# Ordering edges in a hybrid encoder layer: bias tiles behind a row's scaling, and the second half of a mix behind the first half's low parts

## The chip, the cores and the metric

The kernel runs on one core of one Trainium2 chip. A core has five engines that run their own instruction lists side by side: PE (TensorE, matrix products; PEld is its weight load), DVE (VectorE), ACT (ScalarE), POOL (GpSimd) and SP (SyncE, which here only issues transfers, as ACT does for some). Matrix products write to PSUM, a small memory of eight banks; everything else lies in SBUF, and transfers between SBUF and the main memory go through 16 DMA engines. The metric is the time of one execution on the device in microseconds (us); smaller is better.

## The reference, cut to what matters

One encoder layer on 1024 tokens of 1024 channels, in float32: a normalised input goes through one projection whose columns feed two attention groups side by side; their outputs are normalised apart, joined, projected back and added to the input; a gated MLP with a small convolution follows.

```python
hn = rmsnorm(h, norm_mix[l])
proj = jnp.einsum('bsd,de->bse', hn, w_in[l])
qa, ka, va, qb, kb, vb = jnp.split(proj, splits, axis=-1)
...
o_a = window_gqa_sink(qa, ka, va, sink[l])            # 8 heads, window of 128 tokens
o_b = neighbourhood_attention(qb, kb, vb, rpb[l])     # 8 heads, 8 x 16 window on the 16 x 64 grid
mix = jnp.concatenate([rmsnorm(o_a, norm_a[l]), rmsnorm(o_b, norm_b[l])], axis=-1)
h = h + jnp.einsum('bse,ed->bsd', mix, w_out[l])
hn = rmsnorm(h, norm_ffn[l])
h = h + conv_gated_mlp(hn, w_gate[l], w_up[l], conv_w[l], conv_b[l], w_down[l])
return rmsnorm(h, norm_final)
```

In the neighbourhood attention each head adds a learned bias to its scores, taken from a small table by the row and column offset of query and key:

```python
bias = rpb32[:, row_off][:, :, col_off]
s = jnp.einsum('bchd,bicjhd->bhcij', q_r, k_win).astype(jnp.float32) * scale + bias[None]
p = jax.nn.softmax(s.reshape(B, B_HEADS, GRID_W, kh * NA_KW), axis=-1)
```

## The kernel before, in words

**Precision.** Each float32 operand of a product is split into a high part (a rounded copy, made by ACT) and a low part (what is left, made by DVE or POOL); a product is three matmuls, high by high, high by low and low by high. So a matmul of a new operand waits for an ACT instruction and then for a DVE or POOL one.

**Order of the work.** A planner at compile time orders each engine's list; at run time an engine works its list strictly from the front, and a wait at the front holds all behind it. The planner goes by priorities: earlier in the program is more urgent, `tc.high_priority(offset=n)` lifts instructions by n places, and `behind(name)` adds an edge for the order alone: what is traced in its block on the marked instruction's engine comes behind that instruction. PE is different: its order is the order of the program, written by hand (`manual_schedule`). A generator (`filler`) deals out the steps of the projections between those of the attention, so that PE always has a product to work on while softmax goes on elsewhere.

**Attention of group B** (heads 0 to 7, the grid). A head has eight blocks of 128 queries, called rows here, b = 0 to 7. The function `units_grid` gives for each a step `q_step(b)`: the scores (PE, L434), then `softmax`: DVE adds the bias and takes the minimum (L464), ACT takes the exponential with its sum (L468), DVE the reciprocal `sm` (L469). From there a row goes one of two ways by its letter in PATH_B, "QQTQQQTQ". On path T (rows 2 and 6) POOL scales the row (L472), PE transposes it (L496), and ACT and DVE write its high and low parts (L499, L500). On path Q ACT writes the high part (L483), POOL scales a copy (L488) and writes the low part (L489), and a transposing transfer on SP's queue turns both (L490). Then PE multiplies by the values (L598). Up to three units of two rows run ahead of the products that use them.

**Bias tiles.** `bias_tiles(h)` loads head h's part of the table (`rr`, one buffer, L546, on SP's queue) and POOL subtracts it from two masks (L556, 128 x 384, and L557, 128 x 256) into `xb` (two buffers). It is called for head h+1 in `q_step(4)` of head h, and for head 0 early, at unit 8 of group A. Nothing but data and buffers sets when the planner places these two.

**Hand-over.** After the last head: `scale_gains`, the squared sums of group B's four mix tiles and their inverse roots (`vb2`, per token half). Three rows of the output projection's first half (`OutA`, d = 5 to 7, L685 adds the residual) still run as filler. The second heads' mix is then normalised in place (L1129, DVE), copied to a high part (L1130, ACT) and reduced to a low part (L1131, DVE), for token half h = 0 and then h = 1, four tiles each. ACT also squares the eight first raw tiles of the MLP's weights to find their scale (`head_scan`, L1068), and `settle_scales` sums the results (L1035). Then come sixteen products, `product16(ps, wo[d], mg[4:8], h)`, all d with half 0 first, then all d with half 1; `settle_out` adds their results to the residual (L1207). `load_wo` prepares their weights; the low parts (L1104) of d >= 2 stand behind "rows", the last low part of half 0.

The core of the hand-over before the change:

```python
for h in range(2):
    wide = widen(vb2[h], "pt")
    for i in range(4):
        ...
        nc.vector.scalar_tensor_tensor(x, x, gains[:, 4 + i:5 + i], wide, op0=ALU.mult, op1=ALU.mult)
        nc.scalar.activation(hi, x, AF.Copy)
        copied = nc.vector.tensor_tensor(lo, x, hi, op=ALU.subtract)
```

Of the kernel before, what the change touches and what calls it, by code (L numbers as in the profile page):

```python
# [18 lines left out]
ALU = mybir.AluOpType  # L19
# [44 lines left out]
def hybrid_layer(tc, xT, w_in, w_out, w_gate, w_up, w_down, small, sink, rpb, consts, rope, out):  # L64
    nc = tc.nc
    with ExitStack() as ctx:
# [192 lines left out]
        def widen(v, tag, n=4):  # L259

            wide = bank("sw", tag)
            for c in range(n):
                nc.tensor.transpose(wide[:, c * 128:(c + 1) * 128], v[:, c:c + 1].to_broadcast([128, 128]), ident)
            return wide
# [185 lines left out]
        class Rows:  # L450
# [5 lines left out]
            def softmax(self, path, j, ps, n, bias, nsink=None, skip=0):  # L456

                c = n // 128
                with tc.high_priority(offset=50):
                    p = apool.tile([128, 386], F32, name="p", tag="p", bufs=PS)  # L460
                    nm, sm = (spool.tile([128, 1], F32, name=x) for x in ("nm", "sm"))
                    if nsink is not None:
                        nc.gpsimd.tensor_copy(p[:, n:n + 1], nsink)
                    nc.vector.tensor_tensor_reduce(  # L464
                        out=apart(p[:, 0:n]), in0=apart(ps[:, 0:n]), in1=bias, scale=1.0, scalar=3e38 if nsink is None else nsink,
                        op0=ALU.add, op1=ALU.min, accum_out=nm)
                    e = n if nsink is None else n + 1
                    nc.scalar.activation(p[:, 0:e], p[:, 0:e], AF.Exp, bias=nm, scale=-1.0, accum_out=sm)  # L468
                    nc.vector.reciprocal(sm, sm)  # L469
                    x = apart(p[:, 0:n])  # L470
                    if path in "PT":
                        nc.gpsimd.tensor_scalar(x, x, sm, P_TOP, op0=ALU.mult, op1=ALU.mult)  # L472
                    if path == "T":
                        return lambda: self.turn(j, p, c, skip)
                    hl = staged()
                    hi, lo = (hl[:, 0:c, s] for s in range(2))
                    if path == "P":
                        nc.scalar.activation(hi, x, AF.Copy)
                        nc.gpsimd.tensor_tensor(lo, x, hi, op=ALU.subtract)
                    else:  # L480
                        by = spool.tile([128, 1], F32, name="by")
                        nc.vector.tensor_scalar(by, sm, P_TOP, None, op0=ALU.mult)
                        nc.scalar.activation(hi, x, AF.Copy, scale=by)  # L483
                        if path == "D":
                            nc.vector.scalar_tensor_tensor(lo, x, by, hi, op0=ALU.mult, op1=ALU.subtract)
                        else:
                            y = apart(apool.tile([128, 384], F32, name="y", tag="y", bufs=YS)[:, 0:n])
                            nc.gpsimd.tensor_scalar(y, x, sm, P_TOP, op0=ALU.mult, op1=ALU.mult)  # L488
                            nc.gpsimd.tensor_tensor(lo, y, hi, op=ALU.subtract)  # L489
                    mark["flip"] = nc.sync.dma_start(self.tile[:, j, skip:skip + c].rearrange("p i s q -> p (i s) q"), hl[:, 0:c], transpose=True)  # L490
# [51 lines left out]
        def bias_tiles(h):  # L542

            raw = apool.tile([128, RAW_LEN], F32, name="rr", tag="rr", bufs=1)
            src = bass.AP(tensor=rpb.tensor, offset=rpb.offset + h * RPB_LEN, ap=[[RPB_W, ROWS], [1, 8], [1, RAW_LEN]])
            nc.sync.dma_start(raw, src)  # L546
            x = apool.tile([128, 5, 128], F32, name="xb", tag="xb")
            a = raw[:, 0:1]
            view = lambda d0, step, n: bass.AP(
                tensor=a.tensor, offset=a.offset + RAW_LEN - 1 - 8 * (d0 + 1),  # L550
                ap=[list(a.ap[0]), [-8 * step, n], [-RPB_W, ROWS], [-1, 8]])
            mk = cst[:, K_MB:K_MB + 384].rearrange("p (v r c) -> p v r c", r=ROWS, c=8)
            far = mk[:, 1:2]
            far = bass.AP(tensor=far.tensor, offset=far.offset, ap=[list(far.ap[0]), [0, 2], [8, ROWS], [1, 8]])
            xv = x[:, :, :].rearrange("p v (r c) -> p v r c", c=8)
            nc.gpsimd.tensor_tensor(xv[:, 1:4], mk, view(-1, 1, 3), op=ALU.subtract)  # L556
            nc.gpsimd.tensor_tensor(xv[:, 0::4], far, view(-1, 2, 2), op=ALU.subtract)  # L557
            return x

        bias_of = {}  # L560
# [98 lines left out]
        class OutA:  # L659
# [9 lines left out]
            def run(self):  # L669
                d = self.d  # L670
                if d < 6:
                    h1[d] = big("h1", "mix" if d < 4 else "op")
                    xt = tmp("xr")
                    nc.sync.dma_start(xt, xT[d])
                else:
                    for e in range(d, KT):
                        if h1[e] is None:
                            h1[e] = big("h1", "op")
                            mark["xr"] = nc.sync.dma_start(h1[e], xT[e])
                    xt = h1[d]  # L680
                for h in range(2):
                    ps = bank("pj", "pj")
                    yield from product16(ps, self.w, mg[0:4], h)
                    with tc.high_priority(offset=500):
                        nc.vector.scalar_tensor_tensor(h1[d][:, tsl(h)], ps, wo_back, xt[:, tsl(h)], op0=ALU.mult, op1=ALU.add)  # L685

            def post(self):
# [216 lines left out]
        def fill(n):  # L904
            while n > 0 and next(filler, False):
                n -= 1
# [122 lines left out]
        def settle_scales(i, n, tag):  # L1029

            fs = FO[i:i + n]
            n = len(fs)
            rows = (w_rows if i >= HEAD else head_rows)[:, 2 * i:2 * i + 2 * n].rearrange("p (n s) -> p n s", s=2)
            v = small("wv", 4)[:, 0:n]
            nc.vector.tensor_tensor(v, rows[:, :, 0], rows[:, :, 1], op=ALU.add)  # L1035
            s = measure(v, tag)
            back = little(4, "back", "backs", 4)[:, 0:n]
            nc.vector.reciprocal(back, s)  # L1038
            nc.gpsimd.tensor_tensor(back, back, unit_back.to_broadcast([128, n]), op=ALU.mult)  # L1039
            for j, f in enumerate(fs):  # L1040
                taps = little(3, "taps", "taps", 12)
                nc.gpsimd.tensor_scalar(taps, par[:, C_CW + 3 * f:C_CW + 3 * f + 3], back[:, j:j + 1], 1.0, op0=ALU.mult, op1=ALU.mult)
                scale_of[f], back_of[f], taps_of[f] = s[:, j:j + 1], back[:, j:j + 1], taps
# [21 lines left out]

        def head_scan(i, j):
            junk = big("junk", "op")
            nc.scalar.activation(junk[:, :].rearrange("p (k c) -> p k c", c=128), head_raw[FO[i]][j], AF.Square, accum_out=head_rows[:, 2 * i + j:2 * i + j + 1])  # L1068

        W = {}  # L1070

# [24 lines left out]
        def load_wo(d, pools):  # L1096
            raw = wo_raw.pop(d)
            if d % 2 == 0:
                wo_raw["t"] = big("wo", "op").bitcast(F16)[:, :].rearrange("p (d s j c) -> p d s j c", d=2, s=2, c=128)
            t = wo_raw["t"][:, d % 2]  # L1100
            with tc.high_priority(offset=300):
                nc.scalar.activation(t[:, 0], raw, AF.Copy, scale=wo_by)
                with behind(*["rows"] * (d >= 2)):
                    nc.vector.scalar_tensor_tensor(t[:, 1], raw, wo_by, t[:, 0], op0=ALU.mult, op1=ALU.subtract)  # L1104
            return [(t[:, 0, j, :], t[:, 1, j, :]) for j in range(4)]
# [15 lines left out]
                    head_load(i, j)  # L1121
        mg[4:8] = [pairs("mg", "xg") for _ in range(4)]
        gains_up(4)
        for h in range(2):
            wide = widen(vb2[h], "pt")
            for i in range(4):
                x = mix[4 + i][:, tsl(h)]
                hi, lo = mg[4 + i][h]
                nc.vector.scalar_tensor_tensor(x, x, gains[:, 4 + i:5 + i], wide, op0=ALU.mult, op1=ALU.mult)  # L1129
                nc.scalar.activation(hi, x, AF.Copy)  # L1130
                copied = nc.vector.tensor_tensor(lo, x, hi, op=ALU.subtract)  # L1131
                if h == 0:
                    mark["rows"] = copied
            if h == 0:
                wo = [load_wo(d, wpool) for d in range(2)]
                fill(3)
        wo += [load_wo(d, wpool) for d in range(2, 3)]
        while next(filler, None) is not None:
            pass
        for i in range(HEAD):  # L1140
            for j in range(2):
                head_scan(i, j)
        attention_pools.close()


# [750 lines left out]
```

## Time and profile before

| what | before |
|---|---|
| time, median of 3 runs (lowest to highest) | 1035.52 us (1035.21 to 1036.41) |
| the profiled execution's own time | 1035.44 us |
| its span, first to last instruction | 1033.6 us |
| busy: PE, DVE, ACT, POOL | 1011.4, 880.5, 677.1, 215.1 us |
| mean granted PE clock | 0.996 |

Times within the profile count from the first instruction. A row of a timeline gives the start, the duration, the engine, the line of the kernel, the operation, the tile written and the tiles read, the shape, the count of instructions merged into the row, and in brackets the idle time of the engine just before, with what ended it. Matmuls are pipelined, so a row's duration is longer than the step from one start to the next. A "q" behind an engine's name (SPq) is its queue of issued transfers. In the rows of waits stand the total in us, the number of times and the longest.

The stretches of the span that matter below: 20 to 60 us, the first projections and the rotation of their first tiles; 59 to 185, scores of group A; 185 to 355, group B; 355 to 392, the hand-over and the output projection's second half, token half 0; to 417, its token half 1; from 417, the MLP.

### The profile page before, as it was taken

To read this page: it belongs to the slowest core of one execution; us is meant where nothing else is said; L and a number is where in the kernel's file an instruction comes from. 1 tells how busy PE (TensorE), PEld (TensorE's weight loads), DVE (VectorE), ACT (ScalarE), POOL (GpSimd) and SP (SyncE) were. 2 spreads that over 40 slices of the span, in tenths; PEclk is the share of its full clock that TensorE was granted. 3 is DMA by queue.
4 is the path that set the end of the run, shared out by engine and by line. 5 is a ranking of instruction groups with operands and counts; after the bars stand their busy time and mean duration, and the time that the engine had idled before them with its cause. 6 is when DMAs were issued, how large, how long until landed. Compare 5 with 4: busy or idle time off the path is not lost.

```text
span 1033.6 us, 15700 instructions
## 1 busy us (share of the span) xinstructions
PE 1011.4 (98%) x5102; PEld 578.2 (56%) x5102; DVE 880.5 (85%) x1746; ACT 677.1 (66%) x1242; POOL 215.1 (21%) x340
## 2 busy tenths in 40 slices
PE   8989999999999999999999999999999999999996
PEld 6877777777775545544444444444444444444446
DVE  6798988766898699899898988888888879999864
ACT  7557787777687587645778777754535656555551
POOL 1325555676866301000000000000000000000002
PEclk9999999999999999999999999999999999999999
DMA  8566574777689775300687867733232779878734
GB/s 306 201 138 129 106 131 100 149 164 140 139 179 221 233 260 199 112 1 28 219 271 265 278 232 248 252 110 135 83 112 102 247 251 307 306 244 269 260 133 163
DMA packets 143939, 191.80 MB, mean 186 GB/s; under 512 B 77360, under 2 KB 88112, under 8 KB 143856
## 3 DMA queue, kind: packets, MB, share of 16 engines
q1 hardware_dynamic: 133264, 164.84, 55.4%
q10 hardware_dynamic: 10592, 25.95, 6.6%
q8 instruction: 40, 0.66, 0.3%
q14 instruction: 43, 0.35, 0.1%
HBM read 132.81 MB, written 28.57 MB: 156 GB/s over the span
## 4 chain that ended last, share of the span: by engine, by line
PE 73%; DVE 5%; DMA 1%; ACT 1%; issue 1%; POOL 0%; DVEq 0%; ACTq 0%; POOLq 0%
PE dn L1186 6%; PE dn L1185 6%; PE dn L1184 6%; PE pj L180 6%; PE z L1186 5%; PE z L1184 5%; PE z L1185 5%; PE y L1186 4%; PE y L1184 4%; PE y L1185 4%; PE x L1184 4%; PE x L1186 4%; PE x L1185 4%; PE pj L172 2%; PE pj L174 2%; PE pj L173 2%
## 5 line engine op out<-in xcount | busy, mean ns | idle before, releaser
L1186 PEld LDWEIGHTS <-wlo 128*128 128x128 f16 x898 | 87.9, 98 | 101.3
L1184 PEld LDWEIGHTS <-whi 128*128 128x128 f16 x898 | 88.1, 98 | 100.2
L1185 PEld LDWEIGHTS <-whi 128*128 128x128 f16 x898 | 87.9, 98 | 100.3
L1185 PE MATMUL dn<-xd,whi 128*128 128x512 f16 (+1 forms) x330 | 120.4, 365 | 0.0
L1186 PE MATMUL dn<-xd,wlo 128*128 128x512 f16 (+1 forms) x330 | 120.4, 365 | 0.0
L1184 PE MATMUL dn<-xd,whi 128*128 128x512 f16 (+1 forms) x330 | 120.4, 365 | 0.0
L172 PE MATMUL pj<-xgh,whi 128*128 128x512 f32 x248 | 107.3, 433 | 0.0
L468 ACT ACTIVATE p<-p,nm 128x385 f32<-128x385 f32 (+3 forms) x128 | 74.8, 585 | 38.9 <-DVE nm L464 32.1
L1184 PE MATMUL z<-hg,whi 128*128 128x512 f16 x264 | 100.1, 379 | 0.0
L1185 PE MATMUL z<-hg,whi 128*128 128x512 f16 x264 | 100.1, 379 | 0.0
L1186 PE MATMUL z<-hg,wlo 128*128 128x512 f16 x264 | 100.1, 379 | 0.0
L174 PE MATMUL pj<-xgh,wlo 128*128 128x512 f32 x248 | 98.5, 397 | 0.0
L173 PE MATMUL pj<-xgl,whi 128*128 128x512 f32 x248 | 97.9, 395 | 0.0
L1158 ACT ACTIVATE whi<-ws,m 128x512 f16<-128x512 f32 (+1 forms) x96 | 65.8, 708 | 37.1 <-DVE ws L1325 22.6
L1159 DVE SCALAR_TENSOR_TENSOR wlo<-ws,m,whi 128x512 f16<-128x512 f32 (+1 forms) x96 | 70.1, 740 | 16.5 <-ACT whi L1158 16.3
L1039 POOL TENSOR_TENSOR back<-back,cst 128x4 f32<-128x4 f32 (+1 forms) x7 | 2.8, 394 | 356.8 <-DVE back L1038 356.8
L1173 ACT ACTIVATE scan<-scan 128x1024 f32<-128x1024 f32 (+1 forms) x60 | 61.0, 1017 | 16.6 <-DMA scan<-in_w_down_dram 13.7
L1158 ACT ACTIVATE whi<-raw,m 128x512 f16<-128x512 f32 (+1 forms) x78 | 51.4, 699 | 15.7 <-DMA raw<-in_w_down_dram 9.0
L1159 DVE SCALAR_TENSOR_TENSOR wlo<-raw,m,whi 128x512 f16<-128x512 f32 (+1 forms) x78 | 55.4, 731 | 6.4 <-ACT whi L1158 6.2
L1184 PE MATMUL y<-hg,whi 128*128 128x512 f16 x160 | 60.6, 379 | 0.0
L1185 PE MATMUL y<-hg,whi 128*128 128x512 f16 x160 | 60.6, 379 | 0.0
L1186 PE MATMUL y<-hg,wlo 128*128 128x512 f16 x160 | 60.6, 379 | 0.0
(298 smaller groups left out, 2463.8 us busy)
## 6 DMA issues: line engine op xcount, KB each, us to landing
xd<-x SPq DMA_DIRECT2D x77, 256.0 KB, 5.4
raw<-in_w_down_dram SPq DMA_DIRECT2D x64, 256.0 KB, 3.5
x<-c ACTq DMA_DIRECT2D x22, 512.0 KB, 2.8
scan<-in_w_gate_dram SPq DMA_DIRECT2D x18, 512.0 KB, 4.0
scan<-in_w_up_dram SPq DMA_DIRECT2D x18, 512.0 KB, 4.2
raw<-in_w_gate_dram SPq DMA_DIRECT2D x18, 512.0 KB, 4.4
raw<-in_w_up_dram SPq DMA_DIRECT2D x18, 512.0 KB, 3.6
raw<-in_w_in_dram SPq DMA_DIRECT2D x32, 256.0 KB, 3.1
```

The lines of the kernel that those rows point to most:

```text
L172: nc.tensor.matmul(ps, w[0], x[0][:, tsl(h)], start=first, stop=False)
L173: nc.tensor.matmul(ps, w[0], x[1][:, tsl(h)], start=False, stop=False)
L174: nc.tensor.matmul(ps, w[1], x[0][:, tsl(h)], start=False, stop=last)
L180: nc.tensor.matmul(ps, a, b, start=i == 0 and b is x[h][0] and a is w[0], stop=i == len(ws) - 1 and a is w[1])
L468: nc.scalar.activation(p[:, 0:e], p[:, 0:e], AF.Exp, bias=nm, scale=-1.0, accum_out=sm)
L1039: nc.gpsimd.tensor_tensor(back, back, unit_back.to_broadcast([128, n]), op=ALU.mult)
L1158: mark["whi"] = nc.scalar.activation(hi, src, AF.Copy, scale=by)
L1159: nc.vector.scalar_tensor_tensor(lo, src, by, hi, op0=ALU.mult, op1=ALU.subtract)
L1173: nc.scalar.activation(t, t, AF.Square, accum_out=dst)
L1184: nc.tensor.matmul(ps, w[0], x[0], start=first and i == 0, stop=False, skip_group_check=True)
L1185: nc.tensor.matmul(ps, w[0], x[1], start=False, stop=False, skip_group_check=True)
L1186: nc.tensor.matmul(ps, w[1], x[0], start=False, stop=last and i == len(ws) - 1, skip_group_check=True)
```

## The change

Only the order is changed; no computation is added or left out. (1) POOL's scaling of a row on path P or T is marked "scaled", and the two subtractions of a bias tile for heads 1 to 7 stand behind the newest one so marked. (2) The loop over the mix halves becomes a function `normed_b(h, wide)`. Half 0 is traced where it was. Half 1 is traced at the end, behind `head_scan`, lifted by 250 places; its normalisations stand behind "rows", its high copies behind "scanned", the newest square of `head_scan`. The last two squares stand behind "half", the last high copy of half 0. (3) In `OutA` the addition for d = 7, token half 1, stands behind "rows". (4) The sum of two columns at the start of `settle_scales` is lifted by 500 places.

```diff
                     if path in "PT":
-                        nc.gpsimd.tensor_scalar(x, x, sm, P_TOP, op0=ALU.mult, op1=ALU.mult)
+                        mark["scaled"] = nc.gpsimd.tensor_scalar(x, x, sm, P_TOP, op0=ALU.mult, op1=ALU.mult)
...
-            nc.gpsimd.tensor_tensor(xv[:, 1:4], mk, view(-1, 1, 3), op=ALU.subtract)
-            nc.gpsimd.tensor_tensor(xv[:, 0::4], far, view(-1, 2, 2), op=ALU.subtract)
+            with behind(*["scaled"] * (h > 0)):
+                nc.gpsimd.tensor_tensor(xv[:, 1:4], mk, view(-1, 1, 3), op=ALU.subtract)
+                nc.gpsimd.tensor_tensor(xv[:, 0::4], far, view(-1, 2, 2), op=ALU.subtract)
...
-                    with tc.high_priority(offset=500):
+                    with tc.high_priority(offset=500), behind(*["rows"] * (d == KT - 1 and h == 1)):
                         nc.vector.scalar_tensor_tensor(h1[d][:, tsl(h)], ps, wo_back, xt[:, tsl(h)], op0=ALU.mult, op1=ALU.add)
...
-            nc.vector.tensor_tensor(v, rows[:, :, 0], rows[:, :, 1], op=ALU.add)
+            with tc.high_priority(offset=500):
+                nc.vector.tensor_tensor(v, rows[:, :, 0], rows[:, :, 1], op=ALU.add)
...
-            nc.scalar.activation(junk[:, :].rearrange("p (k c) -> p k c", c=128), head_raw[FO[i]][j], AF.Square, accum_out=head_rows[:, 2 * i + j:2 * i + j + 1])
+            mark["scanned"] = nc.scalar.activation(junk[:, :].rearrange("p (k c) -> p k c", c=128), head_raw[FO[i]][j], AF.Square, accum_out=head_rows[:, 2 * i + j:2 * i + j + 1])
...
-        for h in range(2):
-            wide = widen(vb2[h], "pt")
+
+        def normed_b(h, wide):
+
             for i in range(4):
                 x = mix[4 + i][:, tsl(h)]
                 hi, lo = mg[4 + i][h]
-                nc.vector.scalar_tensor_tensor(x, x, gains[:, 4 + i:5 + i], wide, op0=ALU.mult, op1=ALU.mult)
-                nc.scalar.activation(hi, x, AF.Copy)
+                with behind(*["rows"] * h):
+                    nc.vector.scalar_tensor_tensor(x, x, gains[:, 4 + i:5 + i], wide, op0=ALU.mult, op1=ALU.mult)
+                with behind(*["scanned"] * h):
+                    high = nc.scalar.activation(hi, x, AF.Copy)
                 copied = nc.vector.tensor_tensor(lo, x, hi, op=ALU.subtract)
-                if h == 0:
-                    mark["rows"] = copied
             if h == 0:
-                wo = [load_wo(d, wpool) for d in range(2)]
-                fill(3)
+                mark["half"], mark["rows"] = high, copied
+
+        normed_b(0, widen(vb2[0], "pt"))
+        wo = [load_wo(d, wpool) for d in range(2)]
+        fill(3)
+        wide_b = widen(vb2[1], "pt")
         wo += [load_wo(d, wpool) for d in range(2, 3)]
         while next(filler, None) is not None:
             pass
         for i in range(HEAD):
-            for j in range(2):
-                head_scan(i, j)
+            with behind(*["half"] * (i > 2)):
+                for j in range(2):
+                    head_scan(i, j)
+        with tc.high_priority(offset=250):
+            normed_b(1, wide_b)
         attention_pools.close()
```

## The prediction

> **What bounds the kernel now.** I read the page first, then the list of what TensorE waited for, then its busy time by stretches of 20 us, and last the single instructions around each wait. In the fence stand three rows of the stretches (after the two times: their sum, then busy time and instructions of PE, PEld, DVE, ACT and POOL, the granted clock, the DMA share, GB/s) and the rows of the waits (total us, times, longest).
>
> ```profile
> PE 1011.4 (98%) x5102; PEld 578.2 (56%) x5102; DVE 880.5 (85%) x1746; ACT 677.1 (66%) x1242; POOL 215.1 (21%) x340
> ...
> 60.00:80.00 20.00, 16.96 (x75) 13.63 (x74) 18.04 (x54) 11.01 (x27) 7.15 (x17) 0.91 0.70 143
> ...
> 200.00:300.00 100.00, 100.00 (x555) 78.64 (x555) 74.48 (x220) 69.11 (x154) 74.64 (x93) 1.00 0.73 149
> ...
> 360.00:380.00 20.00, 18.66 (x93) 9.08 (x92) 19.34 (x37) 17.67 (x32) 1.80 (x4) 1.00 0.82 319
> ...
> PE pt L496 <- POOL p L472: 3.8, 4, 1.2
> PE s L434 <- DVE hl L485: 3.0, 1, 3.0
> PE pj L180 <- DVE mg L1131: 1.3, 1, 1.3
> PE o L598 <- DMA turned<-stage: 1.1, 1, 1.1
> ...
> PE o L598 <- DMA turned<-hl: 0.5, 1, 0.5
> ```
>
> TensorE is busy 1011.4 of 1033.6 us, and the change neither adds nor removes a matmul nor moves one in TensorE's handwritten order. So it can win only out of 22 us of waits, and lose only by making new ones. Three places can be reached: the wait of 1.3 us for the first low part of the second heads' mix (L1131); the waits of the last heads of group B for a row's scaling or its turned copy (one of the four L472 waits, 1.0 us at 312.87, and those of 0.5 and 1.1); and, less visibly, the wait of 3.0 us near 62.
>
> **The late part: mix halves and last residual.** Here are ACT, DVE and PE at the hand-over (start, duration, engine, line, tile, count, idle before):
>
> ```profile
> 359.99 1.06 ACT L1068 ACTIVATE junk<-rw 128x1024 f32<-128x1024 f32 x1 [1.92 <-DMA rw<-in_w_gate_dram]
> ...
> 365.17 1.06 ACT L1068 ACTIVATE junk<-rw 128x1024 f32<-128x1024 f32 x1 [0.19 <-DMA rw<-in_w_gate_dram]
> ...
> 366.23 1.13 ACT L1130 ACTIVATE mg<-mixb 128x512 f16<-128x512 f32 x2
> ...
> 362.64 2.06 DVE L1129 SCALAR_TENSOR_TENSOR mixb<-mixb,gains,sw 128x512 f32<-128x512 f32 x3
> ...
> 365.39 2.06 DVE L1129 SCALAR_TENSOR_TENSOR mixb<-mixb,gains,sw 128x512 f32<-128x512 f32 x3
> 367.36 0.75 DVE L685 SCALAR_TENSOR_TENSOR h<-pj,wo_back,h 128x512 f32<-128x512 f32 x1
> ...
> 368.09 1.28 DVE L1131 TENSOR_TENSOR mg<-mixb,mg 128x512 f16<-128x512 f32 x2
> ...
> 368.83 0.38 PE L180 MATMUL pj<-mg,wo 128*128 128x512 f16 x1 [1.34 <-DVE mg L1131]
> ```
>
> ACT makes five squares (359.99 to 365.17, one each 1.3 us) and only then the first high part, 366.23 to about 366.8 (1.13 for two). The low part that TensorE waits for could start then, but DVE is still at the second half's normalisation (L1129, until 367.4) and at the last residual addition (L685, until 368.0), and starts it at 368.09. The change puts both behind the four low parts. The first then runs from 366.85 to 367.49 (1.28 for two, 0.64 each), and TensorE, which ran out at 368.83 - 1.34 = 367.49, goes on at about 367.55. **Gain 1.25**. The later low parts follow at 0.64 each, about TensorE's own pace of three matmuls per input tile. Bounds: 1.34 if the first high part comes earlier; nothing if ACT's list gets a sixth square ahead of it (1.3 us later), which the new edges allow, as only the seventh and eighth stand behind the copies ("half").
>
> What waits instead: four L1129 (0.69 each), the residual addition (0.7) and what hangs on them. Against TensorE, DVE is then 4 x 0.69 + 0.7 = 3.4 us later than before. The addition frees a bank that is next written two products on; the second half's mix is first multiplied eight products, of twelve matmuls each, later. So cover exists; what I looked for is where DVE is closest to TensorE afterwards.
>
> ```profile
> 420.08 2.53 DVE L1192 TENSOR_TENSOR hg<-h,hg 128x512 f16<-128x512 f32 x4
> ...
> 427.03 0.16 DVE L1229 TENSOR_SCALAR v<-ss 128x4 f32<-128x4 f32 x1 [2.54 <-PE ss L1224]
> ...
> 422.56 0.38 PE L1184 MATMUL x<-hg,wp 128*128 128x512 f16 x1
> ...
> 398.38 0.75 DVE L1207 SCALAR_TENSOR_TENSOR h<-pj,wo_back,h 128x512 f32<-128x512 f32 x1 [0.66 <-PE pj L180]
> ```
>
> The first of four low parts is done at 420.08 + 0.63 = 420.7 and used from 422.56 on, 1.9 us later. Before it DVE stands idle about 0.6 to 0.7 us four times (one is shown, at 398.38, waiting for TensorE), so some 0.8 us of the 3.4 is left there, under the 1.9; the 2.54 us at 427 swallow the rest. Price 0, bounds 0 to 1.5 (3.4 - 1.9, if nothing were absorbed). The urgent sum of the squares (L1035) is four columns wide, and the additions of residuals hide it.
>
> **The bias tiles.** Two POOL subtractions (L556, L557) make the tiles of head h+1 while head h is at its row 4; the newest marked scaling is then that of row 2 of head h, and the edge holds them behind it. Only heads 1 to 7 get it.
>
> ```profile
> 43.14 1.28 POOL L556 TENSOR_TENSOR xb<-cst,rr 128x384 f32<-128x384 f32 x1 [3.55 <-DMA rr<-in_rpb_dram]
> 44.38 1.18 POOL L557 TENSOR_TENSOR xb<-cst,rr 128x256 f32<-128x256 f32 x1
> ...
> 43.76 1.20 DVE L157 TENSOR_TENSOR wlo<-raw,whi 128x512 fp32r<-128x512 f32 x1
> 44.89 0.94 DVE L289 TENSOR_TENSOR f<-f 64x256 f32<-64x256 f32 x1
> ...
> L157 DVE TENSOR_TENSOR wlo<-raw,whi x16: 670/689/1199, 15.2 to 156.7; 128x512 fp32r<-128x512 f32 x16
> ...
> L289 DVE TENSOR_TENSOR turns<-turns x2: 415/420/426, 52.1 to 101.7; 128x256 f32<-128x256 f32 x2
> ...
> 51.13 0.49 DVE L287 TENSOR_TENSOR turns<-turns 128x128 f32<-128x128 f32 x2 [1.52 <-DMA turns<-t]
> ...
> 59.51 1.21 DVE L299 SCALAR_TENSOR_TENSOR t<-t,q 128x1024 fp32r<-128x1024 f32 x1
> ...
> 60.76 1.16 SPq L302 DMA_DIRECT2D q<-t  x2
> ...
> 65.28 0.36 PE L434 MATMUL s<-ka,q 128*128 128x256 f32 x1 [3.04 <-DVE hl L485]
> ...
> 66.88 0.63 PE L173 MATMUL pj<-xgl,whi 128*128 128x512 f32 x1
> ```
>
> The second pair of all, that of head 1, runs at 43.14 to 45.56, before there is any attention. Two DVE instructions beside it take 1.20 and 0.94 us; the same lines take 0.69 (median) and 0.42 elsewhere, so it costs DVE 0.51 + 0.52 = 1.03 us. DVE's list from there is without slack: the rotated third tile, the transfer that DVE awaits at 51.13, the queries' low part at 59.51, the transfers of 60.76, and then the scores at 65.28, for which TensorE had waited 3.04 us. (The row names L485, on the same list.) Held behind row 2 of head 0 the pair can't run before about 192, and the wait should shrink to 2.0. **Gain 1.03**; bounds 0 (the queries are late for another reason) and 1.03 + 1.7, of which below. The Trainium skill, GPSIMD Engine Reference, section 8 (Key points), says that GpSimd shares its SBUF interfaces with VectorE and contends with instructions that have two SBUF inputs; L157 and L289 have two, and agree. By that rule the price isn't gone but moves to the new place, and the sum would be 1.25 instead of 2.28 if DVE were as pressed there.
>
> At the new place, 192 to 202, the pair (1.74 us by the medians of its two lines, 1.01 and 0.73) is laid into a stretch where POOL works without a gap till 200, but TensorE, which uses what comes out of it some microseconds later, is busy all the time from 200 to 300 (the row above). Price 0, at most 1.74. The table of bias values for head 2 (one transfer on SP) must wait for the pair too, so it leaves SP's queue at 55 and comes back behind 192; head 2's pair comes only ten us later, so I count it nothing. The pairs of heads 2 to 6 land in a gap of POOL behind row 2 of the head before, as here that of head 6 (1.82 us); for head 7's, in head 6, there is only 0.30:
>
> ```profile
> 302.62 0.59 POOL L488 TENSOR_SCALAR y<-p,sm 128x384 f32<-128x384 f32 x1 [1.82 <-DVE sm L469]
> ...
> 310.14 0.99 POOL L556 TENSOR_TENSOR xb<-cst,rr 128x384 f32<-128x384 f32 x1
> 311.09 1.17 POOL L557 TENSOR_TENSOR xb<-cst,rr 128x256 f32<-128x256 f32 x1
> 312.24 0.58 POOL L472 TENSOR_SCALAR p<-p,sm 128x384 f32<-128x384 f32 x1
> ...
> 318.56 0.58 POOL L472 TENSOR_SCALAR p<-p,sm 128x384 f32<-128x384 f32 x1
> 319.44 0.58 POOL L488 TENSOR_SCALAR y<-p,sm 128x384 f32<-128x384 f32 x1 [0.30 <-DVE sm L469]
> ...
> 331.02 6.39 DMA turned<-stage
> ...
> 337.46 0.38 PE o L598 x2
> ```
>
> The scaling at 312.24 moves up to 310.14, and TensorE's wait of 1.02 there goes. But (the last two rows are of the chain of waits) TensorE is stopped again at 337.46 by a turned copy whose transfer leaves at 331.02, after DVE work that has hardly a gap from 311.9 on and doesn't hang on POOL. What is won at 312 is waited for later: **net 0**. Bounds: +2.6 (all three waits, 1.0 + 0.5 + 1.1, gone) and -1.7 (the pair, now at 319, holds up the rows from 319.44 on, and their transfers with them).
>
> **The sum**: 1.25 + 1.03 + 0 = 2.28 us off the profiled execution's 1035.44 us (span 1033.6; the median of the runs is 1035.52, so this execution stands for them): **1033.2**.
>
> **The rivals.** *The clock stays up* (0.16). Behind the wait of 3.04 us matmuls take 0.63 instead of 0.40 for a while, and the clock of that stretch is 0.91, so 0.09 x 20 = 1.8 us are lost; behind the 1.34 us at 367 it is 1.00. A wait of 2.0 lies between. If the clock holds, up to 1.7 more is won: about 1031.5. Against it: what TensorE then wins it may wait for at the next scores, which DVE makes. The Trainium skill, TensorE: Matmul & The Clock Gate, "Why this matters for your kernels", allows no idle gaps above some 3 us before the clock drops; by that rule 2.0 us pass without a drop, and the rows here say nothing on 2.0.
>
> *One of the two gains doesn't come* (0.26): a sixth square on ACT ahead of the copies, or 1.03 us of DVE that something else waits for anyway, as TensorE waits 1.2 us twice between 80 and 120. Then 1034.2 to 1034.4.
>
> *Slower* (0.10): the bias pair of head 7 is put between rows 2 and 3 of the last-but-one head, where POOL, SP's transfers and DVE follow each other closely; TensorE's waits there add up in one place. It decides once that wait is as long as the one at 62: about 3 us and the clock with it (1.8). Then -2.28 + 3.0 + 1.8 = +2.5: 1037.9. For it speaks the missing gap at 319.44; against it that the row shown waits 0.30 for DVE: DVE, not POOL, sets the pace there.
>
> *Nothing* (0.06): both parts come out in the old order or the gains are waited for elsewhere: 1035.4.
>
> **How the numbers follow.** The forecast has 0.42, with 1032.2 to 1034.2 as its own range. What a measurement of this kernel can tell from no change is about 0.2%, 2.1 us; faster by it means below 1033.45, so the forecast lies just past the line. Of its 0.42 I count 0.25 as faster and 0.17 as same; the clock rival is faster (0.16), of the one-gain rival 0.03 is; same has 0.17 + 0.23 + 0.06. Faster 0.44, same 0.46, slower 0.10. The range, 1031.2 to 1036.4, takes in the clock rival, one gain, no gain and a loss of one us (part of the -1.7); only the slower case and the tails stay out.
>
> **What would show it.** Right: the first L1131 starts within 0.1 us of the end of the first L1130, and TensorE's wait for it is below 0.2; DVE's L157 and L289 near 43 take 0.7 and 0.4; the wait at the scores near 62 is about 2.0; no subtraction of a bias tile stands ahead of a scaling that TensorE waits for, but the sum of the waits from 311 to 338 stays near 2.7. Wrong: six squares ahead of L1130; a wait at 62 that is still 3; a wait of TensorE behind 369 that isn't there now, above all at 422; a new wait for a turned copy past 320.

## The result, and the profile after

The changed kernel is slower: 1038.39 us (median of 15 runs, 1037.21 to 1042.42) against 1035.32 (15 runs) on the same chip, ratio 1.0029 with a 95% interval of 1.0021 to 1.0038. Forecast were 1033.2 us, between 1031.2 and 1036.4. The profiled execution took 1037.21 us, its span is 1035.4.

Three points on TensorE cut the span: the first column sum (L263, near 36 us), the long run of matmuls of the second heads' mix, and the first product of the MLP (x). The summary of line L263 (durations, then first and last start; the first row factors are the `v` of it), before and after:

```profile
L263 PE MATMUL sw<-cst,v x40: 272/272/294, 275.9 to 1026.7; 128*128 128x128 f32 x40
L263 PE MATMUL sw<-cst,gains x8: 271/272/273, 36.1 to 36.9; 128*128 128x128 f32 x8
```

```profile
L263 PE MATMUL sw<-cst,v x40: 272/273/295, 274.0 to 1029.0; 128*128 128x128 f32 x40
L263 PE MATMUL sw<-cst,gains x8: 271/273/273, 35.2 to 35.9; 128*128 128x128 f32 x8
```

Single matmuls, before and after:

```profile
368.83 5.12 PE L180 MATMUL pj<-mg,wo 128*128 128x512 f16 x23 [1.34 <-DVE mg L1131]
...
417.38 0.38 PE L1184 MATMUL x<-hg,wp 128*128 128x512 f16 x1
```

```profile
364.62 0.38 PE L180 MATMUL pj<-mg,wo 128*128 128x512 f16 x1 [0.20 <-ACT mg L1135]
365.35 1.02 PE L180 MATMUL pj<-mg,wo 128*128 128x512 f16 x4 [0.35 <-DVE mg L1136]
...
419.27 0.38 PE L1194 MATMUL x<-hg,wp 128*128 128x512 f16 x1
```

| stretch | before | after | difference |
|---|---|---|---|
| to 36 us, where nothing differs | 36.1 | 35.2 | -0.9 |
| to the second heads' mix | 332.7 | 330.2 | -2.5 |
| mix to the MLP's first product | 48.55 | 53.92 | +5.4 |
| to the end of the span | 616.2 | 616.1 | -0.1 |

So the change wins 2.5 us, near the 2.28 of the forecast, and then loses 5.4 in 54 us. The 0.9 at the start is a difference between two executions (in the fourteen profiles of this document the first column sum comes between 35.1 and 36.4 us); without it the two profiles lie 2.7 us apart, as the medians do (3.1). The waits of TensorE in the changed kernel (us in all, times, longest) name the new place:

```profile
PE ss L1234 <- ACT s L1221: 1.9, 1, 1.9
PE s L434 <- DVE nm L464: 1.4, 2, 0.9
PE ss L1234 <- DVE s L1223: 1.3, 1, 1.3
```

`ss`, TensorE's sum of the residuals' squares, hadn't been in my working at all. `settle_out` adds a product to the residual on DVE (L1217), issues its transfer to main memory from ACT's queue (L1218) and squares it on ACT (L1221); the squares of the first four are added up on DVE (L1223), and two products later TensorE sums what came out over the channels (L1234, `sum_up`). The stretch in the changed kernel, TensorE first, then DVE, then ACT:

```profile
375.93 5.34 PE L180 MATMUL pj<-mg,wo 128*128 128x512 f16 x24
382.57 1.02 PE L1234 MATMUL ss<-ones,s 128*128 128x1 f32 x8 [1.30 <-DVE s L1223]
383.46 2.75 PE L180 MATMUL pj<-mg,wo 128*128 128x512 f16 x12
388.09 1.05 PE L1234 MATMUL ss<-ones,s 128*128 128x1 f32 x8 [1.88 <-ACT s L1221]
389.00 4.44 PE L180 MATMUL pj<-mg,wo 128*128 128x512 f16 x12
```

```profile
380.48 0.74 DVE L1106 SCALAR_TENSOR_TENSOR wo<-raw,wo_by,wo 128x512 f16<-128x512 f32 x1
381.15 0.68 DVE L1136 TENSOR_TENSOR mg<-mixb,mg 128x512 f16<-128x512 f32 x1
381.75 0.68 DVE L1223 TENSOR_TENSOR s<-s,s 128x512 f32<-128x512 f32 x1
...
383.01 1.40 DVE L1217 SCALAR_TENSOR_TENSOR h<-pj,wo_back,h 128x512 f32<-128x512 f32 x2
...
386.25 0.75 DVE L1217 SCALAR_TENSOR_TENSOR h<-pj,wo_back,h 128x512 f32<-128x512 f32 x1 [0.52 <-PE pj L180]
```

```profile
379.78 0.61 ACT L1221 ACTIVATE s<-h 128x512 f32<-128x512 f32 x1
...
383.78 0.98 ACTq L1218 DMA_DIRECT2D h1d<-h  x2
384.87 1.06 ACT L1183 ACTIVATE scan<-scan 128x1024 f32<-128x1024 f32 x1 [2.21 <-DVE h L1217]
...
387.03 0.33 ACTq L1218 DMA_DIRECT2D h1d<-h  x1
387.40 0.63 ACT L1221 ACTIVATE s<-h 128x512 f32<-128x512 f32 x1 [1.38 <-DVE h L1217]
```

The fourth residual is squared by 380.4, but DVE first makes a low part of `wo` and one of the second half's mix (L1136), and its sum comes at 381.75 to 382.4; TensorE had asked at 382.57 - 1.30 = 381.27. The fifth residual, whose product TensorE finished about 378.6, is added at 383.01. ACT's list then holds the issues of the fifth and sixth transfers, a scan, the issue of the seventh, and only behind it the fifth square. The seventh can't be issued before TensorE has made its product (DVE, 386.25), so the fifth square starts at 387.40, and TensorE stands still for 1.88 us. In the 12 us from 380 to 392 the granted clock is 0.90, which it is not in the kernel before (the columns as in the prediction's stretches; before, then after):

```profile
380.00:392.00 12.00, 12.00 (x70) 6.90 (x67) 12.00 (x24) 10.50 (x19) 2.02 (x4) 1.00 0.66 223
```

```profile
380.00:392.00 12.00, 8.82 (x43) 4.49 (x42) 11.45 (x20) 8.09 (x15) 5.63 (x6) 0.90 0.65 219
```

The waits make 3.2 of the 5.4 us. The clock makes 1.7: the twelve matmuls behind the second wait take 4.44 us, those behind the first 2.75. The 0.5 that is left lies at the edges of the two waits, where TensorE's instructions don't overlap (a part of it: a sum behind a wait starts 0.89 and 0.91 us ahead of the next matmul, and 0.81 in the kernel before). From the third sum on nothing differs: to the MLP's first product both kernels take 26.00 us (from 391.38 before, from 393.27 after).

### The profile page after: what moved, and what is told of

It reads as the page before. It is cut to its first block, busy times and chain, and to the rows that moved or that the text cites. A ratio compares the mean times of both kernels' runs of the same rounds, so it can differ in the third digit from the quotient of the medians.

```text
span 1035.4 us, 15695 instructions
## 1 busy us (share of the span) xinstructions
PE 1012.6 (98%) x5102; PEld 576.9 (56%) x5102; DVE 879.0 (85%) x1746; ACT 676.6 (65%) x1242; POOL 218.9 (21%) x340
## 4 chain that ended last, share of the span: by engine, by line
PE 69%; DVE 6%; DMA 3%; ACT 2%; issue 1%; SPq 0%; POOL 0%; ACTq 0%; DVEq 0%; POOLq 0%
PE dn L1196 6%; PE dn L1194 6%; PE dn L1195 6%; PE z L1194 5%; PE z L1196 5%; PE z L1195 5%; PE pj L180 4%; PE y L1196 3%; PE y L1195 3%; PE y L1194 3%; PE x L1194 3%; PE x L1196 3%; PE x L1195 3%; PE pj L172 2%; PE pj L174 2%; PE pj L173 2%
```

## The experiments

All medians, with the ratio to the kernel before from runs on the same chip, and the two inner stretches of the table for the profiled execution (in the hand-over alone the first matmul stands in one row with the run, whose start is therefore taken 5.18 us ahead of the next run of 24, as in the other kernels without a slow clock there):

| kernel | median | ratio (95%) | 36 us to mix | mix to MLP |
|---|---|---|---|---|
| changed kernel | 1038.39 | 1.0029 (1.0021 to 1.0038) | 330.2 | 53.92 |
| bias edge alone | 1033.48 | 0.9980 (0.9971 to 0.9989) | 330.1 | 48.55 |
| hand-over alone | 1040.76 | 1.0054 (1.0041 to 1.0066) | 331.1 | 55.59 |
| square first | 1036.75 | 1.0014 (1.0005 to 1.0023) | 330.5 | 52.06 |
| second half unlifted | 1041.59 | 1.0058 (1.0046 to 1.0071) | 329.8 | 57.55 |
| bias edge, head 1 | 1033.99 | 0.9985 (0.9975 to 0.9995) | 332.0 | 48.56 |
| bias edge, heads 2 to 7 | 1034.79 | 0.9990 (0.9981 to 0.9998) | 331.9 | 48.76 |
| sum not lifted | 1043.05 | 1.0073 (1.0058 to 1.0089) | 329.8 | 59.30 |
| residual edge alone | 1034.87 | 0.9998 (0.9989 to 1.0007) | 333.0 | 48.58 |
| bias and residual edges | 1031.90 | 0.9962 (0.9947 to 0.9976) | 331.1 | 48.55 |
| the same again | 1033.00 | 0.9976 (0.9966 to 0.9986) | 331.2 | 50.23 |
| the same, square first | 1032.95 | 0.9978 (0.9969 to 0.9986) | 330.2 | 49.08 |
| square first, sums later | 1034.55 | 0.9996 (0.9987 to 1.0005) | 331.6 | 47.78 |

A profiled execution need not lie at the median of its kernel: that of the residual edge alone took 1037.74 us against 1034.87, that of the repeated pair of edges 1036.13 against 1033.00. So differences of some tenths between two stretches say little.

**The theory**: the bias edge wins, the hand-over wins little and loses 5 us at the sums of squares, because the second half's mix now lies among the residual additions. **Its rival**: the hand-over's list is innocent; TensorE only arrives early in a stretch whose pace DVE sets, and loses its lead there by waiting.

**Bias edge alone.** The kernel before, plus

```diff
+mark["scaled"] = nc.gpsimd.tensor_scalar(x, x, sm, P_TOP, op0=ALU.mult, op1=ALU.mult)
+with behind(*["scaled"] * (h > 0)):
     nc.gpsimd.tensor_tensor(xv[:, 1:4], ...)
     nc.gpsimd.tensor_tensor(xv[:, 0::4], ...)
```

> The kernel before with only the edge on the bias tiles. Theory A (the bias edge wins, the hand-over loses): the traces give 1.0 us won by the first mix of heads (TensorE 0.9 us ahead at 36 us, where nothing differs yet, 1.9 ahead at 275) and 1.0 more between 311 and 340, no new wait at the sums of squares near 384: 2.0 us faster than before, 1033.4. Theory B (the hand-over's list is innocent, TensorE merely arrives earlier at a stretch that DVE sets, and waits its lead off there): new waits at the sums of squares here too, no gain: 1035.4. Theory C (the 0.9 us at the start belong to the change): 1032.5.

Measured: 1033.48, as the theory had it. TensorE arrives at the mix as early as in the changed kernel (365.65 and 365.35), there is no wait at the sums, and the next 48.55 us are the same as before. This is the best measure of what the hand-over changed, since TensorE asks at nearly the same times. Its rows, DVE, ACT and TensorE:

```profile
378.75 0.69 DVE L1214 TENSOR_TENSOR s<-s,s 128x512 f32<-128x512 f32 x1
...
381.41 0.95 PE L1225 MATMUL ss<-ones,s 128*128 128x1 f32 x8
...
384.03 0.61 ACT L1212 ACTIVATE s<-h 128x512 f32<-128x512 f32 x1
...
384.80 0.95 PE L1225 MATMUL ss<-ones,s 128*128 128x1 f32 x8
```

The fourth sum starts at 378.75 here and at 381.75 in the changed kernel, 3.0 us later: nearly the five instructions, of 0.66 us from start to start, that the hand-over's edges put behind the first half's low parts (four normalisations of the second half, one residual addition). It had 381.41 - 379.44 = 2.0 us to spare. The fifth square ends at 384.64 with 0.2 us to spare; in the changed kernel it comes 3.4 us later.

**Hand-over alone.** The changed kernel without the edge on the bias tiles.

> The changed kernel without the edge on the bias tiles. Theory A: the hand-over itself gives 0.7 us at the second heads' mix and loses 5.3 at the sums of squares (waits of 1.3 and 1.9 us, the rest by the lower clock behind them): 4.6 slower than before, 1040.0, with both waits in the profile near 384 and 390. Theory B: TensorE arrives 2 us later, the waits are gone: 1034.7.

Measured: 1040.76, theory A. Both waits are there to the hundredth:

```profile
384.06 1.02 PE L1234 MATMUL ss<-ones,s 128*128 128x1 f32 x8 [1.30 <-DVE s L1223]
384.94 4.44 PE L180 MATMUL pj<-mg,wo 128*128 128x512 f16 x12
391.26 1.36 PE L1234 MATMUL ss<-ones,s 128*128 128x1 f32 x8 [1.88 <-ACT s L1221]
```

TensorE comes 1.5 us later, and the lists are late by as much, since they hang on its products. With the bias edge alone it comes early and doesn't wait: the rival falls. The 1.7 us more than in the changed kernel between mix and MLP are clock: twelve matmuls take 4.44 us behind the first wait, where they took 2.75.

**Square first.** The changed kernel, with

```diff
-nc.scalar.dma_start(spilled[d][:, tsl(h)], at(d, h))
 s2 = half("s2")
 ...
-    nc.scalar.activation(s2, at(d, h), AF.Square)
+    mark["s2"] = nc.scalar.activation(s2, at(d, h), AF.Square)
 ...
+with behind("s2"):
+    nc.scalar.dma_start(spilled[d][:, tsl(h)], at(d, h))
```

> The changed kernel, with each transfer of a residual to DRAM issued behind its own square on ACT (one edge more). DVE's order stays. If the second wait at the sums of squares (1.9 us at 388) is ACT's, whose square of the fifth residual stands behind the issue of the seventh's transfer, which waits for a product TensorE hasn't made: that wait falls to about 0.5, and with it the fall of the clock (1.7): 3 us faster than the changed kernel, 1035.3; the first wait, 1.3, stays. If it is DVE's backlog (the fifth residual is added only at 383): the wait stays above 1.5, time 1038.

Measured: 1036.75, between the two, 1.6 us faster than the changed kernel instead of 3 (the two intervals just touch; from mix to MLP the profiles differ by 1.9). The mechanism was right: the second wait is gone and the clock stays at 1.00. But 1.44 us come back at the row factors, which hang on the last of the sums:

```profile
383.17 1.02 PE L1235 MATMUL ss<-ones,s 128*128 128x1 f32 x8 [1.31 <-DVE s L1222]
384.05 2.75 PE L180 MATMUL pj<-mg,wo 128*128 128x512 f16 x12
386.64 0.95 PE L1235 MATMUL ss<-ones,s 128*128 128x1 f32 x8
...
402.14 0.65 PE L263 MATMUL sw<-cst,v 128*128 128x128 f32 x4 [1.44 <-POOL v L1241]
```

**Second half unlifted.** The changed kernel, with `normed_b(1, wide_b)` called without `tc.high_priority(offset=250)`.

> The changed kernel without the higher priority (250) of the second half's mix. DVE's list then has the last low part of the second half behind the fourth sum of squares and not ahead of it, ACT's list has one scan more ahead of the fifth square. If the first wait (1.3 us at 382) is the low part's place: it falls to 0.7. The second grows by the scan, from 1.9 to 3: in all 1038.9, between 1037.5 and 1040. If the priority is the whole cause of the loss: no waits at the sums, 1034.

Measured: 1041.59, slower than expected. The first wait is 0.70, as it should be with one low part of 0.60 moved behind the sum: so that low part's place makes about half of the first wait. The second is 4.8, not 3: the additional scan ahead of the fifth square also waited for its data.

```profile
382.23 1.02 PE L1233 MATMUL ss<-ones,s 128*128 128x1 f32 x8 [0.70 <-DVE s L1222]
...
388.95 1.06 ACT L1182 ACTIVATE scan<-scan 128x1024 f32<-128x1024 f32 x1 [3.27 <-DMA scan<-in_w_gate_dram]
...
390.67 1.87 PE L1233 MATMUL ss<-ones,s 128*128 128x1 f32 x8 [4.80 <-ACT s L1220]
```

**The bias edge in two.** `h == 1` in place of `h > 0`, and `h > 1`.

> The kernel before with the edge on the bias tiles of head 1 alone (the pair that ran at 43 us). The bias edge as a whole was worth 2.1 us (1033.48 against 1035.59). Theory A (two separate gains, 1.0 where DVE shared with POOL at 43 to 45 us, 1.0 between 311 and 340): 1034.6, and DVE's two instructions there take 0.7 and 0.4. Theory B (the prediction's own terms: 1.03 early, net 0 in the middle): all of it is here, 1033.5.

> The kernel before with the edge on the bias tiles of heads 2 to 7 alone; the pair of head 1 stays at 43 us. Theory A: 1034.6, the waits of TensorE between 311 and 340 fall from 2.7 to 1.5, and the first mix of heads takes as long as before (239.8 us from the first column sums at 36 us to the first row factors at 276). Theory B: 1035.6.

Measured: 1.6 us for head 1 (0.0015 x 1035), 1.0 for the others, each with an interval of 1 us to either side; together 2.6 against 2.1 for both. That is nearer to theory A, and the second is what tells: the prediction had 0 for it. The first can't tell 1.0 from 2.1. With heads 2 to 7 alone the first mix of heads took 240.3 us, not the 239.8 expected; the edge changes nothing there. The waits behind the tables of heads 6 and 7, in the kernel before 1.02, 0.52 and 1.13, are in the run with heads 2 to 7 alone:

```profile
325.74 0.22 PE L599 MATMUL o<-turned,v 128*128 128x128 f16 x1 [0.74 <-DVE turned L500]
329.86 0.55 PE L496 MATMUL pt<-cst,p 128*128 128x128 f32 x3 [0.37 <-POOL p L472]
```

That is 1.1 us in all. In all fourteen profiles the waits of TensorE from 300 to 340 us add up to 1.1 to 1.9 with this edge (ten kernels) and to 2.5 to 2.9 without it (four).

**Sum not lifted.** The changed kernel, with the addition of two columns in `settle_scales` without its `tc.high_priority(offset=500)`.

> The changed kernel without the higher priority of the sum of the weight rows' squares (four columns on DVE). DVE's list then has the second of these sums behind seven more instructions of 0.7 us and behind the fifth low part, while TensorE's list still has the product that reads it after the fourth product of the second heads' mix, at 376. If that lift repairs what the other edges break: TensorE stands there for 5 to 8 us, 1041 to 1047. If it only adds urgent work ahead of the residuals: the waits at the sums of squares shrink, 1037.

Measured: 1043.05; TensorE waits 8.8 us, longer than I expected, for an instruction of 0.15 us:

```profile
PE wm L1018 <- DVE wv L1036: 8.8, 1, 8.8
```

So the lift isn't a gain of its own, it repairs what the edge on the second half does to the list. The edges on "scanned" and "half" do nothing: without these two the planner makes the same lists for all five engines, instruction by instruction.

**Residual edge alone, and with the bias edge.** Of the hand-over only

```diff
-with tc.high_priority(offset=500):
+with tc.high_priority(offset=500), behind(*["rows"] * (d == KT - 1 and h == 1)):
     nc.vector.scalar_tensor_tensor(h1[d][:, tsl(h)], ps, wo_back, xt[:, tsl(h)], ...)
```

> The bias edge on all heads, and of the hand-over only the last residual addition behind the first half's low parts; the second half's normalisation stays ahead of them, as in the kernel before. If the loss of the changed kernel comes from the second half's mix among the residual additions: no waits at the sums of squares, and the wait for the first low part falls from 0.70 to 0.05, the time of the addition: 1032.8. If it comes from the addition or from the low parts in one row: waits at the sums again, 1035 to 1038.

> The kernel before with one edge: the last residual addition behind the first half's low parts; no edge on the bias tiles. The wait for the first low part, 1.34 us, is the end of DVE's list (second half's normalisation, then the addition, 0.66). Theory A (the two parts add up): the wait falls to 0.7 and the time by 0.7, to 1035.0; with the bias edge's 2.1 that makes 2.8 for both. Theory B (the two together are worth more than their sum, as 1031.9 with both says, 4.3 below before): 1033.5 here.

> The bias edge and the edge on the last residual addition once more, on the same chip as the other runs of this set. From 1033.48 for the bias edge alone and 0.65 for the addition: 1032.8 and a ratio to before of 0.9973; if the ratio of 0.9962 repeats, something besides the wait for the first low part is won.

> As the run with the bias edge and the residual addition's edge, with each transfer of a residual issued behind its own square on ACT. There are no waits at the sums of squares to remove there, so nothing to win: the same time within 1 us. If transfers ahead of squares cost something without a wait of TensorE, it is over 1 us faster.

Measured: with the bias edge no waits at the sums, in three runs; so the loss isn't the addition's nor that of four low parts in a row. What is left of the hand-over is the second half's normalisation, traced later and put behind "rows", with the lift that it needs; no run has that part by itself, so it is found by elimination. The edge on the addition alone gives 0.9998, no gain that can be told, though the waits at the mix fell from 1.34 to 0.34 + 0.35 as expected; with the bias edge it gives 0.9962 in the first set and 0.9976 in the second, against 0.9980 for the bias edge alone. Whether it adds anything to the bias edge isn't settled. The order of square and transfer makes no difference here (0.9978). All three beat both kernels, and so does the bias edge alone, the smallest change.

**Square first, sums later.** The changed kernel with the square first and `sum_up(KT * h + d - 3)`. Here the row factors of the first token half leave out the eighth residual's squares, which come one product too late for them; all instructions run.

> The changed kernel with each transfer of a residual behind its square, and with TensorE's sums of squares asked for three products after their residual instead of two. DVE's list has the same work in nearly the same order, so it is as late. If the first wait (1.3 us at 382) is only that TensorE asks for DVE's fourth sum a little too early: no waits at the sums of squares, and of the 3 us by which the changed kernel is slower than before and the 2.8 that its two good parts are worth, all comes back: 1033. If DVE's backlog holds up something else in its turn (the row factors at 400, the banks): a wait of over 1 us there, 1035 to 1037.

Measured: 1034.55, between the two. There is no wait at the sums, and from mix to MLP it takes 47.78 us (0.8 less than the kernel before, because one more sum, a step of 0.81, now stands behind the MLP's first product). Then the backlog shows at another place than the two I named here: the MLP's low parts, where the prediction had looked for it.

```profile
421.74 0.38 PE L1195 MATMUL x<-hg,wp 128*128 128x512 f16 x1 [1.19 <-DVE hg L1202]
```

## Why the prediction was wrong

**The step that failed** is the price of DVE's backlog in the late part: "Against TensorE, DVE is then 4 x 0.69 + 0.7 = 3.4 us later than before ... Price 0, bounds 0 to 1.5". The backlog was sized well, 3.0 us at the fourth sum of squares. What failed is the search for the tightest point. I looked at the operands that the moved work itself makes and at the next operands DVE makes for TensorE, at 422, where 1.9 us are to spare. Between them DVE and ACT make the residuals' squares, which TensorE asks for two products later. The idle time that I counted as cover lies too late as well: of DVE's four gaps only one, 0.62 us at 379, comes ahead of these sums. The trace of before had the answer in three rows, of the fifth residual:

```profile
384.59 0.74 DVE L1207 SCALAR_TENSOR_TENSOR h<-pj,wo_back,h 128x512 f32<-128x512 f32 x1
...
387.12 0.61 ACT L1211 ACTIVATE s<-h 128x512 f32<-128x512 f32 x1
...
387.98 0.95 PE L1224 MATMUL ss<-ones,s 128*128 128x1 f32 x8
```

The square ends at 387.73 and is used at 387.98: 0.25 us to spare, not 1.9. By these rows an estimate of the price is 3.4 - 0.6 - 0.25, some 2.5 us of waiting. Measured in place of "0 to 1.5": 5.4 us, 3.2 as waits, 1.7 by the clock and 0.5 at the edges of the waits. So the sign that I had given, a new wait of TensorE behind 369, came, but not at 422.

A second omission stands behind it: I counted the moved instructions, not what the planner makes of the rest. With the second half's mix in the list, it put one more issue of a transfer ahead of the fifth square, and that issue waits for a product of TensorE's.

**The hand-over's gain of 1.25**: the mechanism was right. Five squares, not six, stand ahead of the first high part, and the first low part starts with the end of it; what is left of the 1.34 is 0.20 + 0.35. Alone, the hand-over's edges win what was forecast: the wait falls from 1.34 to under 0.2, and the stretch to the mix from 332.7 to 331.1. On top of the bias edge less is left to win, 0.6 of waits (0.48 + 0.70 with the bias edge alone), and in these two executions it doesn't reach the mix, 330.2 us with both and 330.1 with the bias edge alone: the changed kernel had waited 0.4 longer between 300 and 340 (1.53 against 1.13). With the residual edge alone the stretch is 333.0, but 0.7 of that comes ahead of the first row factors, where its edge changes nothing.

**The early gain of 1.03**: the price on DVE was right and the gain came, but not on the path that I had named. DVE's two instructions fall to 0.69 and 0.41 us, and from the first column sums to the first row factors the first mix of heads takes 238.8 instead of 239.8 (the first row factors at 274.0 less the first column sum at 35.2, against 275.9 less 36.1); it takes 238.8 to 239.7 in the ten kernels with the edge on head 1 and 239.7 to 240.5 in the four without. In the changed kernel:

```profile
42.50 0.69 DVE L157 TENSOR_TENSOR wlo<-raw,whi 128x512 fp32r<-128x512 f32 x1
43.11 0.41 DVE L289 TENSOR_TENSOR f<-f 64x256 f32<-64x256 f32 x1
...
61.84 0.36 PE L434 MATMUL s<-ka,q 128*128 128x256 f32 x1 [0.63 <-DVE by L482]
...
77.07 0.55 PE L496 MATMUL pt<-cst,p 128*128 128x128 f32 x3 [1.33 <-POOL p L472]
```

The Trainium skill, GPSIMD Engine Reference, section 8, agrees in this place: once POOL is quiet the two instructions of two SBUF inputs take their usual time. In the hand-over alone, without the edge, the pair ran a little later (from 44.30) and beside other instructions: these two took 0.69 and 0.41 there, and two of L287 1.43 instead of 0.47. So the price goes with the pair. That it moves to the new place (the other reading, 1.25 us in all) isn't seen: with the edge on head 1 alone the kernel wins 1.6 us.

The wait at the scores, though, fell from 3.04 to 0.63 and not to 2.0. The queries' transfer left 2.7 us earlier, counted from the first column sum (57.10 less 35.17, against 60.76 less 36.14): DVE's wait for the turned tile ahead of it (L287) had fallen from 1.52 to 0.57 too, and two of L310 took 2.46 instead of 3.45. What was won beyond 1.0 TensorE waited for again, 1.4 us for DVE (`nm`) and 1.33 for POOL's scaling at 77 (row above), a wait that the kernel before hasn't there. That the sum came out at the 1.03 of the forecast is in part luck.

**The middle, "net 0"**: wrong by 1.0 us, on the good side. The waits from 311 to 338 fell from 2.7 to 0.74 + 0.33 + 0.46 = 1.5, and the edge on heads 2 to 7 alone is worth 1.0 (0.2 to 2.0 by its interval). The argument was that what is won at 312 is waited for at 337, because DVE has hardly a gap there. Half of it wasn't. So that the first 330 us won 2.5, near the 2.28 of the forecast, is luck too: this term was too low, and the hand-over's 1.25 hardly showed beside the bias edge.

**The rivals.** The clock stays up behind the wait near 62, as the first rival had it, but the time it priced (1.7) isn't won: in the run of the hand-over alone the clock stays at 1.00 there too, and the stretch to 275 takes 239.7 us, against 239.8 before with 0.79. What TensorE won by the clock it waited for at 78 us (1.10 us for a scaling on POOL, L472), which is what the prediction held against this rival. Two more kernels with 0.79 (the residual edge alone, and heads 2 to 7) took 240.5 and 240.3, so up to 0.7 us may hang on the clock. The slower rival had the sign and nearly the time (1037.9), but by luck: its place, the bias pair of head 7, holds no longer wait than before: they got shorter there.

## What to carry to other kernels

When instructions are put off on an engine that is full, price them at every use that the engine's list feeds before it catches up, small side products included, and take the smallest slack: compare the end of each producer with the start of its consumer in the trace of before. With a list made by a planner, an edge moves more than it names, on other engines too; a change of several edges should be timed edge by edge, since one may pay for another. An engine that issues transfers and also computes makes whatever stands behind an issue wait for that transfer's data: here a square of 0.6 us stood behind the issue for the seventh residual, and TensorE waited 1.88 us for it.

## What the runs showed of the hardware

What makes the clock fall was less plain than I had it. At the first scores near 62 the kernel before waits 3.04 us and the hand-over alone 2.97; the clock behind it (64 to 72 us) is 0.79 in the first and 1.00 in the second. The stretch of the kernel before, then the wait and the stretch of the hand-over alone:

```profile
64.00:72.00 8.00, 6.72 (x25) 5.60 (x26) 6.36 (x19) 3.71 (x10) 2.72 (x8) 0.79 0.52 105
```

```profile
65.23 0.36 PE L434 MATMUL s<-ka,q 128*128 128x256 f32 x1 [2.97 <-DMA q<-t]
```

```profile
64.00:72.00 8.00, 6.76 (x33) 5.78 (x34) 6.97 (x21) 3.94 (x10) 2.72 (x8) 1.00 0.53 106
```

The Trainium skill, TensorE: Matmul & The Clock Gate, "Why this matters for your kernels", allows gaps up to some 3 us; these two waits agree, and so do 3.09 and 3.10 in the residual edge alone and in heads 2 to 7 (clock 0.79 from 64 to 72 us). The later ones don't: behind a wait of 1.30 us twelve matmuls take 4.44 us in the hand-over alone, behind 1.31 in the square-first kernel they take 2.75, at the same place of the program. When the bias and residual edges were run again, a wait of 1.46 for the mix and one of 0.35 a matmul later were followed by 23 matmuls in 6.81 us; behind the 1.34 of the kernel before they took 5.12. What else decides, these runs don't show.
